# Weight sums and low weight halves made by accumulating DMAs in the output projections of a two-layer trunk

## The chip, the cores and the metric

The kernel runs on one core of one Trainium2 chip. The metric is device time in microseconds (us) of one launch. A core has TensorE (PE in the profile; its weight loads are PEld), VectorE (DVE), ScalarE (ACT), GpSimd (POOL) and SyncE (SP). Transfers are issued by an engine's queue (SPq, POOLq, ACTq) and moved by 16 DMA engines that all queues share. Those issued by SP are called hardware_dynamic in the profile, those issued by POOL software_dynamic.

## The reference, cut to what matters

One step of a diffusion trunk: 128 prompt tokens and 512 sample tokens, model width 2048, two layers. Each layer normalizes and modulates its input, projects it into heads and gates, mixes tokens (windowed attention and a short convolution in layer 0, differential and dense attention in layer 1), and sends the concatenated branches through one output projection, whose gated result is added to the input:

```
y = concat([y_first, y_second], axis=-1)   # 640 tokens x 2048
x = x + gate * (y @ w_out)                 # w_out is 2048 x 2048
```

The change is in `y @ w_out` of both layers. All arrays are float32.

## The kernel before, in words

**Exactness.** TensorE multiplies float32r. To keep float32 accuracy each operand is split into a high part (rounded by a copy into float32r) and a low part (the rest): `split` (L240 to L242) makes `hi` on ACT and `lo = x - hi` on DVE. A product takes three matmuls, high x high, high x low, low x high. `split_w` (L260) does this for 128x512 float32 of weights (four row tiles of 128x128) into `wh` and `wl`, from a pool with four buffers of each.

**Layout.** Activations are kept transposed: 16 row tiles of 128 features x 640 tokens. The tokens are cut into two halves of 320 columns (`HALF`), since an accumulator holds 512 float32.

**Output projection, single tiles.** `project_out` (L1098) makes 16 output tiles (`n`) of 128 features. Tiles 0, 1, 2 are the lead tiles: `run_tiles` loads y back from DRAM (`ydram`, tile `yin`) quarter by quarter, splits it into `h`, and runs the three tiles on each quarter as it comes. Then tiles 3 to `n0 - 1` follow one by one (L1126), each 16 row tiles x 2 halves x 3 = 96 matmuls. Their weights come in quarters of 256 KB (`load_raw`, tile `raw`, four buffers, SP queue), split three quarters ahead (`SPLIT_AHEAD`). `n0` is `N_SINGLE`: 4 in layer 0, 6 in layer 1.

**Output projection, pairs.** The other tiles are made two at a time by `run_pairs` (L431): a 2x2 block product with seven block products in place of eight. With A11, A12, A21, A22 the weight blocks (1024 rows x 128 columns, 512 KB; first index the tile, second the upper or lower half of the rows) and B11 to B22 blocks of the activations, the seven are Q1 (A11), Q2 (A12), N5 (A21 + A22), P6 (N5 + A11), P7 (A11 + A21), P4 (A22) and Q3 (P6 + A12). Each is 8 row tiles x 3 = 24 matmuls of 320 columns. The sums of activations (`T`, four forms) are made once per layer by `forms` (L1045), a generator that `advance(attn, ...)` steps through during the lead and single tiles. The sums of weights are made on DVE in `operand` (L455): N5 in two halves of 128x512 into `sx`, P6 and Q3 as 128x1024 added into `sx`, P7 as 128x1024 into `sf`. Each block of weights is loaded once per pair by SP (L438, A22 by L254).

**Order around the change.** Each engine works in program order. `ahead(s)` (L483) is called after each half product (a step) and makes the operands and splits up to three halves ahead; a split has to wait for one of the four `wh` and `wl` buffers, that is for PE to have finished four halves earlier. After each product, `after` (L490) combines accumulators on DVE in four scratch areas (`room`, tile `tables`), and `done` and `res_sum` (L1080) add the gated result to the residual `xr`, which `res_load` (L1076) fetched. In layer 0 the sum is stored by POOL (L1194) and squared for the next norm; in layer 1 it is transposed back by PE (`rows_out`, L1419), copied by ACT and stored by POOL (L1424, L1425). In layer 0 `x1_tail` (L1234) starts to fetch the sums back into freed operand buffers during the last pair.

Of the kernel before, what the change touches and what calls it, by code (L numbers as in the profile page):

```python
# [53 lines left out]
def trunk_kernel(ctx: ExitStack, tc: tile.TileContext, I: dict, O: dict):  # L54
# [185 lines left out]
    def split(hi, lo, x):  # L240
        A.activation(hi, x, AF.Copy)  # L241
        V.tensor_sub(lo, x, hi)  # L242
# [9 lines left out]
    def load_raw(w_ap, col, qd, js=(0, 4)):  # L252
        raw = wpool.tile([P, js[1] - js[0], P], F32, tag="raw", name="raw")
        nc.sync.dma_start(raw, w_ap[(qd * 4 + js[0]) * P:(qd * 4 + js[1]) * P, col:col + P]  # L254
                          .rearrange("(k p) n -> p k n", p=P))
        return raw

    mark = [None]

    def split_w(raw):  # L260
        wh = wpool.tile(raw.shape, F32R, tag="wh", name="wh")
        wl = wpool.tile(raw.shape, F32R, tag="wl", name="wl")
        split(wh, wl, raw)
        mark[0] = wl[:, 0, 0:1]
        return wh, wl

# [28 lines left out]
    def drain(queue):  # L295
        while queue:
            advance(queue, 1)
# [133 lines left out]
    def run_pairs(cols, w_ap, mov, room, begin, part, done, tail):  # L431

        ap = pools["cur"]
        W8 = KT // 2

        def load8(tag, col, k0, bufs):
            t = ap.tile([P, W8, P], F32, tag=tag, name=tag, bufs=bufs)
            nc.sync.dma_start(t, w_ap[k0 * P:(k0 + W8) * P, col:col + P].rearrange("(k p) n -> p k n", p=P))  # L438
            return t

        st8 = {}

        def load(p, name):
            if p >= len(cols):
                return
            c0, c1 = cols[p]
            if name == "A22":
                st8[p, name] = [load_raw(w_ap, c1, qd) for qd in (2, 3)]
            else:
                st8[p, name] = load8("w8", c1 if name == "A21" else c0, 8 if name == "A12" else 0, 4)  # L450

        def halves(t):
            return [t[:, 0:4, :], t[:, 4:8, :]]

        def operand(p, name):  # L455
            a = lambda n: st8[p, n]
            if name == "Q1":
                return halves(a("A11"))
            if name == "N5":
                x = st8["x"] = ap.tile([P, W8, P], F32, tag="sx", name="sx", bufs=1)  # L460
                for i in range(2):
                    V.tensor_add(halves(x)[i], halves(a("A21"))[i], a("A22")[i])
                return halves(x)
            if name == "P6":
                V.tensor_add(st8["x"], st8["x"], a("A11"))
                f = st8["f"] = ap.tile([P, W8, P], F32, tag="sf", name="sf", bufs=1)
                V.tensor_add(f, a("A11"), a("A21"))
                return halves(st8["x"])
            if name == "Q2":
                return halves(a("A12"))  # L470
            if name == "Q3":
                V.tensor_add(st8["x"], st8["x"], a("A12"))
                return halves(st8["x"])
            if name == "P7":
                return halves(st8["f"])
            return a("A22")

        MOV = {"Q1": "B11", "Q2": "B21", "N5": "T1", "P6": "T2", "P7": "T3", "P4": "T4", "Q3": "B22"}
        seq = [(p, n) for p in range(len(cols)) for n in MOV]
        ops, parts = {}, {}  # L480
        q1, z, u2, u4 = room

        def ahead(s):  # L483
            while len(parts) < min(s + SPLIT_AHEAD, 2 * len(seq)):
                i = len(parts)
                if i % 2 == 0:
                    ops[i // 2] = operand(*seq[i // 2])
                parts[i] = split_w(ops[i // 2][i % 2])

        def after(p, name, ps):  # L490
            if name == "Q1":
                A.copy(q1, ps)
                begin(p)
            elif name == "Q2":
                V.tensor_add(z, ps, q1)
                done(p, 0, 0, z)
            elif name == "N5":
                st8["n5"] = ps
            elif name == "P6":
                V.tensor_sub(u2, ps, q1)  # L500
                V.tensor_sub(u4, st8["n5"], u2)
                if p == len(cols) - 1:
                    part(p, 0, 1, u4)
            elif name == "P7":
                V.tensor_sub(z, ps, u4)
                done(p, 1, 1, z)
                V.tensor_add(u2, ps, u2)
                part(p, 1, 0, u2)
            elif name == "P4":
                done(p, 1, 0, ps)  # L510
            elif p == len(cols) - 1:
                done(p, 0, 1, ps)
            else:
                V.tensor_add(u4, ps, u4)
                done(p, 0, 1, u4)

        for n in ("A11", "A12", "A21", "A22"):
            load(0, n)
        ahead(0)
        for i, (p, name) in enumerate(seq):  # L520
            ps, rows_ = pproj.tile([P, 512], F32, tag=f"p{'ab'[i % 2]}{i // 2 % 2}", name="pq")[:, 0:HALF], mov[MOV[name]]
            for h in range(2):
                wh, wl = parts[2 * i + h]
                for j in range(4):
                    hi, lo = rows_(4 * h + j)
                    PE.matmul(ps, wh[:, j, :], hi, start=(h == 0 and j == 0), stop=False)  # L526
                    PE.matmul(ps, wh[:, j, :], lo, start=False, stop=False)  # L527
                    PE.matmul(ps, wl[:, j, :], hi, start=False, stop=(h == 1 and j == 3))  # L528
# [5 lines left out]
            if name == "Q1":  # L534
                load(p + 1, "A11")
            elif name == "P7":
                load(p + 1, "A12")
            elif name == "P4":
                load(p + 1, "A21")
                load(p + 1, "A22")  # L540
            if name in ("P6", "P7") and p == len(cols) - 1:
                tail(name)
            slot()

# [487 lines left out]
    for _ in fill0:  # L1032
        pass

    N_SINGLE = (4, 6)
    room = [tables[:, i * HALF:(i + 1) * HALF] for i in range(4)]
    W_OUT = [I["ev_w_out"][0], I["od_w_out"][0]]
    T, t1 = [], []
# [1 line left out]
    def big(tag, shape=(P, NT), dtype=F32, bufs=1):  # L1040

        n = 6 * HALF if tag[0] == "T" else 8 * P
        return pools["cur"].tile([P, n], dtype, tag=tag, name=tag, bufs=bufs)

    def forms():  # L1045

        f = None

        def load(j):
            ts = [big("w8", bufs=4)[:, 0:NT] for _ in range(2)]  # L1050
            for i in range(2):
                nc.sync.dma_start(ts[i], ydram[j + 8 * i])
            return ts

        T.clear()
        t1.clear()
        nxt = load(0)
        for j in range(8):
            (ya, yb), nxt = nxt, (load(j + 1) if j < 7 else None)
            b11, b12, b21, b22 = ya[:, 0:HALF], ya[:, HALF:NT], yb[:, 0:HALF], yb[:, HALF:NT]  # L1060
            x = big("sx")[:, 0:3 * HALF]
            if f is None:
                f = big("sf")
# [34 lines left out]
    def project_out(l, maker, finish, last, tail):  # L1098
# [3 lines left out]
        def job(n):  # L1102
            def f(pp):
                res_load(l, n)
                for i in range(2):
                    res_sum(l, n, pp[i], CS[:1] if i == 0 else CS[1:])
                yield
                finish(n)
            return f

        n0 = N_SINGLE[l]
        go_on = run_tiles([(n * P, job(n)) for n in range(3)], w, maker, order=(0, 2, 1, 3))


# [43 lines left out]
        def done(p, t, h, src):  # L1158
# [4 lines left out]
            elif n in seen:  # L1163
# [336 lines left out]
```

## Time and profile before

| | |
|---|---|
| time, median of 3 runs | 2329.14 us (2328.17 to 2330.53) |
| the profiled execution's own time | 2333.26 us |
| its span | 2331.3 us |
| granted TensorE clock, mean | 0.996 |
| data moved by DMA | 321.96 MB |
| pairs of layer 0 | from 980 us to 1130 us of the span |
| pairs of layer 1 | from 2199 us to 2328 us of the span |

The span is what the hardware profiler recorded of one execution. A row of a group reads: line, engine, operation, what it writes <- what it reads, shape, count | busy us in all, mean ns of one | idle time of the engine ahead of it and what ended most of it. A row in order of time starts with start and length in us; a bracket at its end is the idle time of the engine before it and what ended it. Matmuls are pipelined, so that their listed lengths overlap.

### The profile page before, as it was taken

How to read it: one execution, taken by the hardware profiler on the slowest of the kernel's cores; microseconds unless marked ns; L12 is line 12 of the kernel's file. 1: busy time of each engine (PE TensorE's matmuls, PEld its weight loads, DVE VectorE, ACT ScalarE, POOL GpSimd, SP SyncE). 2: the span in 40 equal slices, each digit the busy share in tenths (PEclk: the TensorE clock that was granted, in tenths of full speed). 3: DMA queues.
4: the chain of work that ended last, by engine and by line, in shares of the span. 5: the costliest groups of instructions: out<-in, count | busy, mean ns of one | idle time of the engine just before them, and what ended most of it. 6: DMA issues, size and time to landing. Idle time of an engine off the chain costs nothing.

```text
span 2331.3 us, 41439 instructions
## 1 busy us (share of the span) xinstructions
PE 2286.6 (98%) x15988; PEld 2210.0 (95%) x15988; DVE 1572.5 (67%) x3196; ACT 929.2 (40%) x1935; POOL 133.0 (6%) x181
## 2 busy tenths in 40 slices
PE   7999999999999999999999999999999999999999
PEld 5699999999999999999999999999999999999999
DVE  4559886786876663988855755755756754567576
ACT  4235442433422222544554344444334444444343
POOL 1001000000000000000010100101000001000101
PEclk9999999999999999999999999999999999999999
DMA  9984545445355443844431422413423312128642
GB/s 315 354 267 131 162 116 170 139 119 169 116 180 162 151 139 114 277 142 128 160 98 53 135 82 72 143 52 100 118 72 95 104 46 82 46 74 270 181 122 70
DMA packets 390630, 321.96 MB, mean 138 GB/s; under 512 B 18402, under 2 KB 336368, under 8 KB 389920
## 3 DMA queue, kind: packets, MB, share of 16 engines
q1 hardware_dynamic: 382496, 288.98, 40.9%
q0 software_dynamic: 7216, 28.16, 3.3%
q8 instruction: 126, 2.06, 0.4%
q10 hardware_dynamic: 720, 2.16, 0.3%
q14 instruction: 72, 0.59, 0.1%
HBM read 290.79 MB, written 28.44 MB: 137 GB/s over the span
## 4 chain that ended last, share of the span: by engine, by line
PE 88%; DMA 4%; DVE 4%; ACT 2%; issue 1%; POOL 0%; SPq 0%; ACTq 0%; DVEq 0%; POOLq 0%
PE pa L276 10%; PE pb L277 10%; PE pb L276 10%; PE pb L278 10%; PE pa L277 10%; PE pa L278 10%; PE pq L526 4%; PE pq L528 4%; PE pq L527 4%; PE T L704 2%; PE S L716 1%; PE S L718 1%; PE S L717 1%; DMA yin<-yd 1%; PE T L178 1%
## 5 line engine op out<-in xcount | busy, mean ns | idle before, releaser
L241 ACT ACTIVATE wh<-raw 128x512 fp32r<-128x512 f32 (+1 forms) x490 | 303.1, 620 | 794.7 <-PE pb L277 655.3
L242 DVE TENSOR_TENSOR wl<-raw,wh 128x512 fp32r<-128x512 f32 (+1 forms) x490 | 330.8, 676 | 351.3 <-ACT wh L241 326.1
L276 PE MATMUL pa<-h,wh 128*128 128x320 f32 x1760 | 560.6, 319 | 4.5 <-ACT h L241 3.2
L277 PE MATMUL pa<-h,wh 128*128 128x320 f32 x1760 | 547.3, 312 | 1.8 <-DVE h L242 1.8
L278 PE MATMUL pa<-h,wl 128*128 128x320 f32 x1760 | 546.4, 310 | 0.0
L278 PE MATMUL pb<-h,wl 128*128 128x320 f32 x1760 | 545.4, 310 | 0.0
L276 PE MATMUL pb<-h,wh 128*128 128x320 f32 x1760 | 545.0, 310 | 0.0
L277 PE MATMUL pb<-h,wh 128*128 128x320 f32 x1760 | 544.8, 310 | 0.0
L213 DVE SCALAR_TENSOR_TENSOR acc<-adaw,sT,acc 128x512 f32<-128x512 f32 (+1 forms) x600 | 357.4, 639 | 13.1 <-DMA adaw<-in_ada_w 12.4
L276 PEld LDWEIGHTS pa<-h,wh 128*128 128x128 f32 x1760 | 331.9, 189 | 24.0 <-issue 14.7
L277 PEld LDWEIGHTS pa<-h,wh 128*128 128x128 f32 x1760 | 332.6, 189 | 6.3 <-DVE h L242 2.7
L278 PEld LDWEIGHTS pa<-h,wl 128*128 128x128 f32 x1760 | 332.1, 189 | 1.2 <-issue 1.2
L278 PEld LDWEIGHTS pb<-h,wl 128*128 128x128 f32 x1760 | 330.8, 188 | 2.1 <-issue 2.1
L276 PEld LDWEIGHTS pb<-h,wh 128*128 128x128 f32 x1760 | 330.6, 188 | 1.0 <-issue 0.4
L277 PEld LDWEIGHTS pb<-h,wh 128*128 128x128 f32 x1760 | 330.8, 188 | 0.2
L690 ACT ACTIVATE p<-S,nm,rq 128x768 f32<-128x768 f32 (+3 forms) x120 | 101.2, 844 | 114.8 <-DVE nm L685 81.1
L526 PE MATMUL pq<-h,wh 128*128 128x320 f32 x352 | 110.0, 313 | 0.4 <-DVE xr L1083 0.4
L527 PE MATMUL pq<-h,wh 128*128 128x320 f32 x352 | 108.8, 309 | 0.0
L528 PE MATMUL pq<-h,wl 128*128 128x320 f32 x352 | 108.4, 309 | 0.0
L683 DVE TENSOR_REDUCE nm<-S 128x1 f32<-128x768 f32 (+3 forms) x120 | 91.9, 766 | 16.1 <-PE S L718 14.9
L241 ACT ACTIVATE pth<-T 128x512 fp32r<-128x512 f32 (+1 forms) x132 | 65.9, 533 | 71.4 <-PE T L704 71.3
L527 PE MATMUL pq<-T,wh 128*128 128x320 f32 x264 | 81.4, 308 | 0.0
(303 smaller groups left out, 3382.5 us busy)
## 6 DMA issues: line engine op xcount, KB each, us to landing
raw<-in_od_w_in SPq DMA_DIRECT2D x208, 256.0 KB, 2.8
raw<-in_ev_w_in SPq DMA_DIRECT2D x196, 256.0 KB, 3.0
adaw<-in_ada_w SPq DMA_DIRECT2D x192, 256.0 KB, 3.0
ada<-in_ada_w SPq DMA_DIRECT2D x14, 2048.0 KB, 11.0
adaw<-in_ada_w SPq DMA_DIRECT2D x128, 128.0 KB, 2.3
yd<-y POOLq DMA_DIRECT2D x34, 320.0 KB, 2.8
yin<-yd SPq DMA_DIRECT2D x32, 320.0 KB, 4.8
w<-yd SPq DMA_DIRECT2D x32, 320.0 KB, 4.4
```

The source lines that it names most:

```text
L213: V.scalar_tensor_tensor(out=a, in0=w, scalar=sT[:, kt, c:c + 1], in1=a, op0=ALU.mult, op1=ALU.add)
L241: A.activation(hi, x, AF.Copy)
L242: V.tensor_sub(lo, x, hi)
L276: PE.matmul(ps, wh[:, i, :], hi[:, sl], start=(j == js[0] if alone else (pos == 0 and j == 0)), stop=False)
L277: PE.matmul(ps, wh[:, i, :], lo[:, sl], start=False, stop=False)
L278: PE.matmul(ps, wl[:, i, :], hi[:, sl], start=False, stop=(j == js[1] - 1 if alone else (pos == 3 and j == 3)))
L526: PE.matmul(ps, wh[:, j, :], hi, start=(h == 0 and j == 0), stop=False)
L527: PE.matmul(ps, wh[:, j, :], lo, start=False, stop=False)
L528: PE.matmul(ps, wl[:, j, :], hi, start=False, stop=(h == 1 and j == 3))
L683: V.tensor_reduce(nm, s, axis=AX.X, op=ALU.max, negate=True)
L690: A.activation(p[:, 0:n], s, AF.Exp, scale=rsc, bias=nm, accum_out=l)
L704: PE.transpose(t[:, i * P:(i + 1) * P], p, ident)
```

## The change

Three things change.

1. While `project_out` runs, `split_w` makes `wl` in another way: ACT writes `wh`, ACT writes `wl = -wh`, and a DMA issued by POOL adds the raw weights to `wl`. This holds for the lead tiles, the fourth tile and the pairs.
2. In `run_pairs` each of the seven operands has a 512 KB buffer of its own turn (`r0` to `r5`, six in rotation) and is loaded by SP from DRAM, up to five ahead. Sums are made by accumulating DMAs issued by POOL: N5 adds A22 and P7 adds A21 from DRAM, P6 adds the N5 buffer and Q3 adds the P6 buffer. `forms` and `x1_tail` use these buffers in place of `w8`, `sx` and `sf`.
3. `N_SINGLE` is 4 in both layers, so that layer 1 has six pairs and one single tile behind its lead tiles.

```
-    mark = [None]
+    mark, by_dma = [None], [False]
...
-        split(wh, wl, raw)
+        if by_dma[0]:
+
+            A.activation(wh, raw, AF.Copy)
+            A.activation(wl, wh, AF.Copy, scale=-1.0)
+            nc.gpsimd.dma_start(wl, raw, accum_op=ALU.add)
+        else:
+            split(wh, wl, raw)
...
+        def src8(col, k0):
+            return w_ap[k0 * P:(k0 + W8) * P, col:col + P].rearrange("(k p) n -> p k n", p=P)
+
+        turn = [0]
+
+        def load(p, name):
+
+            c0, c1 = cols[p]
+            col, k0, add = {"Q1": (c0, 0, None), "Q2": (c0, 8, None), "N5": (c1, 0, (c1, 8)), "P6": (c0, 0, "N5"),
+                            "P7": (c0, 0, (c1, 0)), "P4": (c1, 8, None), "Q3": (c0, 8, "P6")}[name]
+            t = ops[p, name] = big(f"r{turn[0] % 6}").rearrange("p (k n) -> p k n", k=W8)
+            turn[0] += 1
+            nc.sync.dma_start(t, src8(col, k0))
+            if add is not None:
+                nc.gpsimd.dma_start(t, src8(*add) if isinstance(add, tuple) else ops[p, add], accum_op=ALU.add)
...
         def ahead(s):
+            while len(ops) < min((s + 1) // 2 + 5, len(seq)) and len(ops) < len(parts) // 2 + 6:
+                load(*seq[len(ops)])
             while len(parts) < min(s + SPLIT_AHEAD, 2 * len(seq)):
                 i = len(parts)
-                if i % 2 == 0:
-                    ops[i // 2] = operand(*seq[i // 2])
-                parts[i] = split_w(ops[i // 2][i % 2])
+                h = ops[seq[i // 2]][:, i % 2 * 4:i % 2 * 4 + 4, :]
+                parts[i] = split_w(h)
...
-    N_SINGLE = (4, 6)
+    N_SINGLE = (4, 4)
...
         n0 = N_SINGLE[l]
+        by_dma[0] = True
...
         drain(prep)
+        by_dma[0] = False
...
-        for k in (range(0, 4) if name == "P6" else range(4, 6)):
-            x1_back(k, big("w8", bufs=4) if k < 4 else big("sx" if k == 4 else "sf"))
+        for k in {"P6": (0, 1, 2, 3), "P7": (4,), "P4": (5,)}[name]:
+            x1_back(k, big(f"r{k}"))
```

More of the change, by code (lines that the diff above doesn't have):

```diff
@@ L434, in run_pairs @@
         W8 = KT // 2
[L436 to L439, printed above, removed]
-        st8 = {}
[L443 to L476, printed above, removed]
@@ L478, in run_pairs @@
-        MOV = {"Q1": "B11", "Q2": "B21", "N5": "T1", "P6": "T2", "P7": "T3", "P4": "T4", "Q3": "B22"}
+        def src8(col, k0):
[10 more added lines that the diff above has]
+                nc.gpsimd.dma_start(t, src8(*add) if isinstance(add, tuple) else ops[p, add], accum_op=ALU.add)
@@ L479, in run_pairs @@
+        MOV = {"Q1": "B11", "Q2": "B21", "N5": "T1", "P6": "T2", "P7": "T3", "P4": "T4", "Q3": "B22"}
+        st8 = {}
         seq = [(p, n) for p in range(len(cols)) for n in MOV]
@@ L515, in after @@
                 done(p, 0, 1, u4)
-        for n in ("A11", "A12", "A21", "A22"):
-            load(0, n)
         ahead(0)
@@ L533, in run_pairs @@
             ahead(2 * i + 2)
[L534 to L541, printed above, removed]
+            if name in ("P6", "P7", "P4") and p == len(cols) - 1:
                 tail(name)
@@ L1049, in load @@
         def load(j):
-            ts = [big("w8", bufs=4)[:, 0:NT] for _ in range(2)]
+            ts = [big(f"r{j % 2 * 2 + i}")[:, 0:NT] for i in range(2)]
             for i in range(2):
@@ L1060, in forms @@
             b11, b12, b21, b22 = ya[:, 0:HALF], ya[:, HALF:NT], yb[:, 0:HALF], yb[:, HALF:NT]
-            x = big("sx")[:, 0:3 * HALF]
+            x = big("r4")[:, 0:3 * HALF]
             if f is None:
-                f = big("sf")
+                f = big("r5")
             d = room[j] if j < 4 else f[:, (j - 4) * HALF:(j - 3) * HALF] if j < 7 else b11
```

## The prediction

> **What bounds the kernel now.** I read four views: busy times and slices of the page, then the groups by line, then a table of time windows (us from the span's start, busy time of each engine with its instructions, granted clock, share of the 16 DMA engines, GB/s), then instructions in order of time inside one pair.
>
> ```profile
> PE 2286.6 (98%) x15988; PEld 2210.0 (95%) x15988; DVE 1572.5 (67%) x3196; ACT 929.2 (40%) x1935; POOL 133.0 (6%) x181
> ...
> L526 PE MATMUL pq<-h,wh 128*128 128x320 f32 x352 | 110.0, 313 | 0.4 <-DVE xr L1083 0.4
> L527 PE MATMUL pq<-h,wh 128*128 128x320 f32 x352 | 108.8, 309 | 0.0
> L528 PE MATMUL pq<-h,wl 128*128 128x320 f32 x352 | 108.4, 309 | 0.0
> ```
> ```profile
> 1003.30:1027.90 24.60, 24.60 (x170) 24.60 (x169) 20.55 (x35) 10.50 (x18) 1.06 (x2) 1.00 0.47 140
> ...
> 2171.00:2199.00 28.00, 28.00 (x194) 27.80 (x193) 13.43 (x25) 9.81 (x20) 2.57 (x4) 1.00 0.48 136
> ...
> 2250.00:2275.70 25.70, 25.70 (x180) 25.68 (x179) 19.15 (x33) 10.54 (x19) 2.57 (x4) 1.00 0.44 132
> ```
>
> TensorE bounds it. Columns after the length are PE, PEld, DVE, ACT, POOL, clock, DMA share, GB/s. The first window is one pair of layer 0, the last one pair of layer 1, the middle one two single tiles of layer 1. PE is never idle in them and the clock is full. DVE is the next engine (20.55 of 24.60 us), yet PE waited for it 0.4 us in all pairs together. So whatever is taken off DVE in the pairs is worth at most that. DMA is below half.
>
> One trap: a matmul's listed 309 ns is not its price, as matmuls overlap. A pair is 7 products x 8 row tiles x 3 = 168 matmuls in 24.60 us, 0.146 us each.
>
> **The change part by part.**
>
> *Six pairs instead of five in layer 1.* Two single tiles (2 x 96 matmuls) become one pair (168): 24 matmuls at 0.146 us, **-3.5 us**. This is the whole gain in sight, since the row transposes and residual sums of a tile stay the same.
>
> *DVE.* Per pair 14 subtractions, two half sums and three whole sums go. They lay beside PE; I cost them at **0** (at most the 0.4 us above). Nothing that PE waits for is behind them.
>
> *ACT.* Each split gets a second activation.
>
> ```profile
> 976.84 1.15 ACT L241 ACTIVATE wh<-w 128x512 fp32r<-128x512 f32 x2 [1.02 <-DMA w<-in_ev_w_out]
> ```
>
> Two back to back take 1.15 us, so 14 more add 14 x 0.575 = 8.1 us to ACT's 10.50 in a pair: 18.6 of 24.60. It fits, **0**. In the lead tiles three more of them stand before the activations that make `h`, 1.7 us per unit of 10.5 us of matmuls; hidden while DMA lasts longer there, and it does (below).
>
> *POOL.* It issues all accumulating DMAs, in order.
>
> ```profile
> 1003.28 0.54 POOL L1194 DMA_DIRECT2D xd<-xr  x1 [21.34 <-DVE xr L1083]
> ...
> 2247.96 0.76 POOL L1424 DMA_DIRECT2D out_y_sample<-ot  x1 [20.36 <-ACT ot L1423]
> ```
>
> An issue of 128 rows takes 0.54 us, one of 512 pieces 0.76. A sum from DRAM has 1024 pieces; by the same slope 1.05 us. A pair gets 16 x 0.54 + 2 x 1.05 = 10.7 us of issues more: room enough. But the DMA that makes operand N5, P6, P7 or Q3 waits on POOL for its plain load to land, and the `wl` DMAs of the coming steps, and the stores of `xr`, stand behind it.
>
> *The path from a free buffer to wl.* Before, `wl` came 0.7 us behind `wh`. Now it is ACT, ACT, POOL, DMA.
>
> ```profile
> 1040.66 0.19 PEld L526 LDWEIGHTS pq<-T,wh 128*128 128x128 f32 x1
> ...
> 1040.92 0.63 ACT L241 ACTIVATE wh<-sf 128x512 fp32r<-128x512 f32 x1 [1.13 <-PE pq L527]
> ...
> 1040.95 0.19 PEld L528 LDWEIGHTS pq<-T,wl 128*128 128x128 f32 x1
> ...
> 1042.62 0.64 ACT L241 ACTIVATE wh<-raw 128x512 fp32r<-128x512 f32 x1 [1.07 <-PE pq L527]
> ```
> ```profile
> yd<-y POOLq DMA_DIRECT2D x34, 320.0 KB, 2.8
> ...
> xd<-xr POOLq DMA_DIRECT2D x16, 320.0 KB, 3.6
> ...
> out_new_c_k<-kg POOLq DMA_DIRECT2D x8, 64.0 KB, 1.9
> ```
>
> A half product (step) lasts 12 x 0.146 = 1.76 us. The split of the part for step n+3 starts 0.26 us into step n, when PE releases the buffer (four buffers; the bracket shows ACT already waits for that). PE wants `wl` 0.29 us into step n+3, that is 3 x 1.76 + 0.29 = 5.57 us after step n began. The path is 0.26 + 1.15 + landing. No row shows an accumulating DMA; plain stores from POOL land 1.9 us (64 KB) to 3.6 us (320 KB) after issue. For 256 KB I take 2.9: 4.3 us. It fits, with **1.3 us to spare**, if nothing is ahead of it in the queue.
>
> *DMA bytes.* Here it does not fit. Per pair, before: four operands of 0.524 MB, two residuals in and two out of 0.328 MB, 3.4 MB (140 GB/s x 24.6 us agrees). After: seven operand loads and two sums from DRAM (4.72 MB), two sums from SBUF (1.05), 14 `wl` of 0.262 MB (3.67), residuals and stores (1.31): **10.75 MB**. In 24.6 us that is 437 GB/s.
>
> ```profile
> 58.00:116.00 58.00, 52.96 (x368) 37.06 (x369) 29.07 (x66) 16.64 (x31) 0.00 (x0) 0.97 1.01 355
> 10.00:20.00 10.00, 7.00 (x33) 5.38 (x34) 5.07 (x14) 4.97 (x9) 1.14 (x2) 0.93 1.02 398
> ```
> ```profile
> q0 software_dynamic: 7216, 28.16, 3.3%
> ```
>
> Where all 16 engines are busy they moved 355 GB/s over 58 us, 398 at best. So a pair takes at least 10.75 / 0.398 = 27.0 us. Counted by busy shares instead: before, 0.47 x 24.6 = 11.6 us of full engines, 297 GB/s; the 2.62 MB more from DRAM at that rate are 8.8 us, the 4.72 MB inside SBUF at POOL's rate (28.16 MB in 3.3% of 2331.3 us: 366 GB/s) 12.9; sum 33.3 us. These are the prices if an accumulating byte costs what a plain one does.
>
> It can hardly cost that: a sum needs its destination read too, which is a second pass over 5.77 MB. With it, 16.5 MB per pair: 41.5 us at 398 GB/s, 46.5 at 355, by the shares (33.3 + 5.77 at about 355) 49.6. The upper end would be that each accumulating DMA is served alone: 14 x 2.9 + 4 x 3.6 = 55 us. Between 27.0 and 55 I take **41.5 us**: two passes at the best rate that the trace shows, since nearly half the first pass and all of the second stay in SBUF.
>
> The Trainium skill ("Collectives: The Full Stack", The bandwidth ceiling) says of adding transfers that the addition is free but the two source reads share one ring, and gives 32.35 against 62.28 GB/s for the copy, a factor of 1.93. No run here shows that yet; by it the two-pass price holds and the one-pass price does not.
>
> *Lead tiles and the fourth tile.* Their 16 quarters per layer also get `wl` by DMA, 4.19 MB, 8.4 with two passes.
>
> ```profile
> 966.00:980.00 14.00, 14.00 (x97) 13.95 (x96) 13.57 (x30) 9.14 (x17) 1.31 (x3) 1.00 0.99 313
> 2113.00:2124.00 11.00, 11.00 (x77) 11.00 (x77) 6.97 (x10) 6.41 (x10) 0.00 (x0) 1.00 0.81 284
> 2124.00:2135.00 11.00, 11.00 (x77) 11.00 (x77) 9.26 (x17) 4.89 (x7) 0.00 (x0) 1.00 0.91 285
> 2135.00:2146.00 11.00, 10.45 (x71) 10.18 (x71) 9.83 (x16) 5.73 (x9) 0.00 (x0) 1.00 0.95 305
> 2146.00:2157.00 11.00, 10.42 (x74) 10.15 (x73) 10.41 (x22) 4.22 (x7) 1.06 (x2) 1.00 0.85 262
> 2157.00:2171.00 14.00, 13.76 (x96) 13.50 (x95) 9.55 (x18) 5.08 (x9) 2.82 (x5) 1.00 1.04 329
> ```
>
> DMA is already full there: the 58 us of layer 1 leave (11 x 0.48 + 14 x -0.04) = 4.7 us of engines free, layer 0, with a like last stretch, I put at the same. 8.4 MB at 398 GB/s are 21 us; 21 - 4.7 = 16 us per layer, **+32 us** in two (one pass: 10.5 - 4.7, +12).
>
> *Sum, against the profiled execution* (2333.26 us, its span 2331.3 with 2.0 around it): layer 0 pairs 6 x (41.5 - 24.6) = +101; layer 1 pairs 6 x (41.5 - 25.7) = +95; lead tiles +32; sixth pair -3.5. Together +225, or 2558. The median of the runs shown, 2329.14, is 4 us below the profiled one, so I say **2554 us**.
>
> **The rivals.**
>
> *One pass, and the queue.* Accumulating costs what copying does. Then a pair is 27.0 to 33.3 us by bytes, and the look-ahead adds: four operand sums per pair stand ahead of a `wl` with an issue of 0.54 to 1.05 us and 0.524 / 0.398 = 1.3 us of transfer; beyond the 1.3 us to spare each costs PE about 1 us. At 31 (27.0 + 4) to 33.3 us: 6 x (6.4 to 8.7) + 6 x (5.3 to 7.6) + 12 - 3.5, which is +79 to +106: about **2420**. For it: packet times of DRAM loads may overlap with SBUF traffic (share 1.04 above). Against: the destination must be read.
>
> *Served one by one.* If an accumulating DMA holds the software queue until it lands, 55 us per pair: 6 x 30.4 + 6 x 29.3 + 32 - 3.5 = +386, **2715**. For it: one POOL queue, in order, with waits for loads inside. Against: q0's stores now move at 366 GB/s.
>
> *It hides.* The other side: the engines deliver the 437 GB/s, and each accumulating DMA lands within 2.9 + 1.3 = 4.2 us of its issue; from there on PE waits for nothing in the pairs, only -3.5 us is left, **2326**. It decides at 437 GB/s in the pair windows. Against: the best 10 us of this trace had 398. By the Trainium skill ("DMA: Bandwidth & Descriptors", Where 436 GB/s comes from) the 16 ports allow 435 GB/s, which would make a one-pass pair 24.7 us and is this rival; the trace's 398 is below it.
>
> **How the numbers follow.** Forecast (two passes) 0.50, its own range 2500 to 2625 (41.5 less a tenth, to 46.5 us per pair). One pass 0.27, one by one 0.14, hidden 0.09. The range runs from 2395 (one pass with 30 us per pair) to 2690; left out are the hidden case and most of the one-by-one case. About 0.2% (4.7 us) is what a measurement of this kernel can tell from no change. -3.5 us is inside it: same 0.06.
>
> ```profile
> L276 PE MATMUL pa<-h,wh 128*128 128x320 f32 x1760 | 560.6, 319 | 4.5 <-ACT h L241 3.2
> L277 PE MATMUL pa<-h,wh 128*128 128x320 f32 x1760 | 547.3, 312 | 1.8 <-DVE h L242 1.8
> ```
>
> To be faster, part of the 3.2 + 1.8 us that PE waits for `h` in the lead tiles would have to go as well: 0.03. Slower 0.91.
>
> **What would show it.** In the pair windows the DMA share should be near 1.0, a pair last about 41 us, PE idle ahead of L528 with `wl` and a DMA as releaser, DVE fall from 20.6 us per pair to about 6, ACT rise to about 18.6. Software queue bytes should go from 28 to about 106 MB (200 `wl` and 48 operand sums). Landing of `wl` well above 4.2 us shows the look-ahead broken. Wrong would be: a DMA share below 0.9 with PE idle (then it is the queue's order or latency, not bytes), or PE without idle time in the pairs (it hides).

## The result and the profile after

The changed kernel takes **2652.62 us** (median of four runs, 2650.25 to 2654.87) where the kernel before takes 2329.84 (2328.17 to 2331.46): a ratio of 1.139 with a 95% interval of 1.137 to 1.140. Its profiled execution took 2654.87 us, with a span of 2651.9. The forecast was 2554, range 2395 to 2690.

Some lines have moved: the pairs' matmuls are now L506 to L508 (before L526 to L528), the lead tiles' L282 to L284, `wh` and `-wh` on ACT L265 and L266, the DMA that completes `wl` L267, an operand's load L454, its sum L456.

From the page after: busy times, the software queue, four groups (busy us, mean ns | idle before it and what ended it), and the landing of `wl` (median us from issue).

```profile
PE 2382.2 (90%) x15964; PEld 2283.2 (86%) x15964; DVE 1405.3 (53%) x2954; ACT 1055.1 (40%) x2142; POOL 367.9 (14%) x429
...
q0 software_dynamic: 64432, 105.77, 20.8%
...
L284 PE MATMUL pb<-h,wl 128*128 128x320 f32 x1728 | 537.3, 311 | 5.7 <-DMA wl<-raw 5.7
...
L508 PE MATMUL pq<-h,wl 128*128 128x320 f32 x384 | 143.3, 376 | 122.2 <-DMA wl<-r 122.0
...
L267 POOL DMA_DIRECT2D wl<-r x168 | 176.0, 1337 | 156.6 <-ACT wl L266 146.3
L508 PE MATMUL pq<-T,wl 128*128 128x320 f32 x288 | 102.9, 358 | 74.6 <-DMA wl<-r 74.5
...
wl<-r POOLq DMA_DIRECT2D x168, 256.0 KB, 7.7
```

PE, never idle in the pairs before, now waits 122.2 + 74.6 = 196.8 us there ahead of the one matmul that reads `wl`, and what ends the wait is the DMA that completes `wl`. It lands 7.7 us after its issue, where the path had room for 4.2. In the lead tiles (L284) the same wait is small.

The table of time windows after: one pair of layer 0, then one stretch of layer 1.

```profile
1093.60:1142.30 48.70, 31.17 (x171) 29.33 (x171) 7.34 (x15) 19.21 (x32) 18.27 (x21) 0.86 1.09 222
...
2440.00:2490.00 50.00, 32.50 (x178) 31.18 (x178) 5.70 (x13) 19.17 (x33) 20.00 (x22) 0.84 1.02 205
```

A pair takes 48.7 us instead of 24.6. DVE has fallen to 7.3 us and ACT risen to 19.2. PE is idle for 17.5 us, and its busy time has grown too, from 24.6 to 31.2 us for the same 168 matmuls: the clock column stands at 0.86. So of 24.1 us more, 17.5 are waits and 6.6 are PE at a slower clock.

The clock in steps of 2 us, with PE's weight loads there in order of time (the bracket is the wait before).

```profile
1064.00:1066.00 2.00, 2.00 (x16) 2.00 (x15) 0.61 (x2) 1.47 (x3) 0.00 (x0) 1.00 1.15 310
1066.00:1068.00 2.00, 1.30 (x9) 1.03 (x8) 0.43 (x1) 1.50 (x3) 1.65 (x3) 1.00 0.71 139
1068.00:1070.00 2.00, 0.59 (x4) 0.59 (x5) 0.00 (x0) 0.19 (x1) 1.85 (x3) 1.00 1.06 197
1070.00:1072.00 2.00, 2.00 (x10) 2.00 (x8) 0.00 (x0) 0.33 (x1) 0.00 (x0) 0.52 1.04 172
1072.00:1074.00 2.00, 1.22 (x5) 0.82 (x5) 0.00 (x0) 0.93 (x2) 0.74 (x1) 0.50 1.13 189
...
1078.00:1080.00 2.00, 2.00 (x16) 2.00 (x15) 0.98 (x2) 1.27 (x2) 0.47 (x1) 1.00 1.14 300
```
```profile
1066.85 0.19 PEld L507 LDWEIGHTS pq<-h,wh 128*128 128x128 f32 x1
1069.40 0.19 PEld L508 LDWEIGHTS pq<-h,wl 128*128 128x128 f32 x1 [2.37 <-DMA wl<-r]
...
1070.64 0.33 PEld L506 LDWEIGHTS pq<-h,wh 128*128 128x128 f32 x1
1070.91 0.33 PEld L507 LDWEIGHTS pq<-h,wh 128*128 128x128 f32 x1
```

After a wait of 2.37 us the granted clock falls to 0.50, and the loads follow each other at 0.27 us instead of 0.146.

One pair seen from POOL, in order of time, shows the order that the queue imposes.

```profile
1112.51 0.85 POOL L267 DMA_DIRECT2D wl<-r  x1 [7.25 <-PE pq L507]
1114.89 0.85 POOL L456 DMA_DIRECT2D r<-r  x1 [1.53 <-DMA r<-in_ev_w_out]
1115.42 2.98 POOL L267 DMA_DIRECT2D wl<-r  x3
...
1130.43 1.57 POOL L456 DMA_DIRECT2D r<-in_ev_w_out  x1 [4.52 <-issue]
```

POOL stands at the sum until the operand's plain load has landed; then three `wl` DMAs come in one burst behind it.

**The sum.** By the start of one sum to the start of the same sum of the next pair, a pair of layer 0 takes 48.6 us (1066.35 to 1260.86 over four pairs) and one of layer 1 51.6 (2415.40 to 2621.95). Six pairs of layer 0 are 6 x 24.0 = 144 us more; six pairs of layer 1 stand in place of five of 25.7 and two single tiles of 28.0 together, 309.6 - 156.5 = 153. By this count 26 of the 323 us are left for the lead and fourth tiles and the edges. But the pairs at the ends are not as long as those between. From the first matmul of the pairs to the start of their last one, layer 0 takes 295.4 us (989.9 to 1285.3) instead of 149.8 (980.2 to 1130.0), which is 145.6 more. Layer 1 takes 300.5 (2346.2 to 2646.7) instead of 129.3 (2197.1 to 2326.4) and 28.0 for the two single tiles, which is 143.2 more. So about 32 of the 320.6 us between the two spans lie outside the pairs: 9.7 ahead of those of layer 0, and 21.8 between the two layers' pairs once the two single tiles are taken out.

### The profile page after: what moved, and what is told of

The parts are those of the page before. It is cut to its first block, busy times and chain, and to the rows that moved or that the text cites. A ratio compares the mean times of both kernels' runs of the same rounds, so it can differ in the third digit from the quotient of the medians.

```text
span 2651.9 us, 41966 instructions
## 1 busy us (share of the span) xinstructions
PE 2382.2 (90%) x15964; PEld 2283.2 (86%) x15964; DVE 1405.3 (53%) x2954; ACT 1055.1 (40%) x2142; POOL 367.9 (14%) x429
## 3 DMA queue, kind: packets, MB, share of 16 engines
q0 software_dynamic: 64432, 105.77, 20.8%
## 4 chain that ended last, share of the span: by engine, by line
PE 65%; DMA 24%; DVE 4%; issue 3%; ACT 2%; POOL 1%; SPq 0%; POOLq 0%; ACTq 0%; DVEq 0%
DMA wl<-r 9%; PE pa L282 8%; PE pb L282 8%; PE pb L283 8%; PE pb L284 8%; PE pa L283 8%; PE pa L284 8%; DMA r<-in_ev_w_out 4%; DMA r<-in_od_w_out 4%; PE T L677 2%; DMA r<-yd 1%; PE S L689 1%; PE S L691 1%; PE S L690 1%; PE T L178 1%
## 5 line engine op out<-in xcount | busy, mean ns | idle before, releaser
L282 PE MATMUL pa<-h,wh 128*128 128x320 f32 x1728 | 551.3, 320 | 9.5 <-ACT h L241 8.2
L241 ACT ACTIVATE wh<-raw 128x512 fp32r<-128x512 f32 (+1 forms) x428 | 264.2, 619 | 736.6 <-PE pb L283 625.2
L283 PE MATMUL pa<-h,wh 128*128 128x320 f32 x1728 | 538.7, 312 | 4.6 <-DVE h L242 4.4
L284 PE MATMUL pb<-h,wl 128*128 128x320 f32 x1728 | 537.3, 311 | 5.7 <-DMA wl<-raw 5.7
L284 PE MATMUL pa<-h,wl 128*128 128x320 f32 x1728 | 537.0, 311 | 3.3 <-DMA wl<-raw 3.3
L282 PE MATMUL pb<-h,wh 128*128 128x320 f32 x1728 | 537.3, 311 | 0.0
L283 PE MATMUL pb<-h,wh 128*128 128x320 f32 x1728 | 536.6, 311 | 0.0
L242 DVE TENSOR_TENSOR wl<-raw,wh 128x512 fp32r<-128x512 f32 (+1 forms) x428 | 288.4, 675 | 333.0 <-ACT wh L241 308.3
L282 PEld LDWEIGHTS pa<-h,wh 128*128 128x128 f32 x1728 | 326.1, 189 | 30.5 <-issue 14.7
L284 PEld LDWEIGHTS pb<-h,wl 128*128 128x128 f32 x1728 | 326.4, 189 | 8.5 <-DMA wl<-raw 6.4
L284 PEld LDWEIGHTS pa<-h,wl 128*128 128x128 f32 x1728 | 326.4, 189 | 5.4 <-DMA wl<-raw 4.1
L282 PEld LDWEIGHTS pb<-h,wh 128*128 128x128 f32 x1728 | 326.2, 189 | 1.0 <-issue 0.4
L508 PE MATMUL pq<-h,wl 128*128 128x320 f32 x384 | 143.3, 376 | 122.2 <-DMA wl<-r 122.0
L265 ACT ACTIVATE wh<-r 128x512 fp32r<-128x512 f32 x168 | 105.7, 631 | 354.9 <-PE pq L507 320.1
L508 PEld LDWEIGHTS pq<-h,wl 128*128 128x128 f32 x384 | 90.7, 237 | 132.4 <-DMA wl<-r 132.3
L267 POOL DMA_DIRECT2D wl<-r x168 | 176.0, 1337 | 156.6 <-ACT wl L266 146.3
L508 PE MATMUL pq<-T,wl 128*128 128x320 f32 x288 | 102.9, 358 | 74.6 <-DMA wl<-r 74.5
L506 PE MATMUL pq<-h,wh 128*128 128x320 f32 x384 | 139.7, 364 | 0.7 <-DVE xr L1056 0.7
```

Source lines behind the costliest of these rows:

```text
L265: A.activation(wh, raw, AF.Copy)
L267: nc.gpsimd.dma_start(wl, raw, accum_op=ALU.add)
L282: PE.matmul(ps, wh[:, i, :], hi[:, sl], start=(j == js[0] if alone else (pos == 0 and j == 0)), stop=False)
L283: PE.matmul(ps, wh[:, i, :], lo[:, sl], start=False, stop=False)
L284: PE.matmul(ps, wl[:, i, :], hi[:, sl], start=False, stop=(j == js[1] - 1 if alone else (pos == 3 and j == 3)))
```

## The experiments

Two theories stood at the start: **full engines** (the bytes of all transfers, destination reads included, fill the 16 DMA engines) and **the queue** (the accumulating DMAs go through one software queue in order, behind waits, and land too late, though the engines have room). A third comes from the critical chain inside a pair after the change (start us, us, what):

```profile
1097.88 10.01 DMA wl<-r
...
1107.95 6.40 DMA r<-in_ev_w_out
...
1115.96 7.12 DMA wl<-r
...
1123.23 6.06 DMA r<-in_ev_w_out
```

It runs from a load through its sum to `wl` and on to the next load, three times per pair: **the loop** (an operand's buffer is released by the DMA that reads it, which lets the next load start).

Each is compared with the kernel before on its own chip; lengths of pairs are those of layer 0, from sum to sum. The diffs are against the kernel before for e1, e4, e8 and e12, and against the changed one for the others.

### e1: six pairs alone

```
-    N_SINGLE = (4, 6)
+    N_SINGLE = (4, 4)
```

> The kernel before with only the sixth pair in layer 1 (single tiles 4 and 4); all sums and low halves stay on VectorE. Both theories of the loss (full DMA engines, or the order of the software queue) expect the 24 matmuls less and nothing else: 3.5 us less, about 2326 us. Rival: VectorE, busy 20.6 of 24.6 us in a pair, or the sums of activations that now have to be ready two tiles earlier, hold TensorE up in layer 1: 2329 us or more, with idle time of TensorE at the start of the pairs.

2334.70 us against 2333.01, ratio 1.0005 (0.9996 to 1.0015). The 3.5 us are not there. Time windows of it around the start of layer 1's pairs, then DVE's work on the first operand in order of time:

```profile
2155.00:2165.00 10.00, 9.02 (x53) 9.02 (x54) 9.37 (x21) 6.55 (x16) 3.88 (x6) 0.83 0.96 291
...
2170.00:2175.00 5.00, 2.68 (x18) 2.23 (x16) 3.15 (x5) 0.63 (x1) 0.00 (x0) 1.00 0.38 97
```
```profile
2171.84 1.29 DVE L462 TENSOR_TENSOR sx<-w,raw 128x512 f32<-128x512 f32 x2 [2.94 <-DMA w<-in_od_w_out]
```

By this trace the two single tiles had been cover. DVE makes the forms beside the lead tiles (9.37 of 10 us busy) and the first operands' loads must wait for the buffers that the forms use; with one single tile left PE arrives earlier, loses about 1 us, then 2.3, and the clock dips to 0.83. These waits and the clock are of the size of the 24 matmuls saved. That the missing cover is the cause is argued from the trace: e8 and e12, below, were to relieve DVE there, and neither brought the gain.

### e2: sums by DMA, wl on DVE

```
-        by_dma[0] = True
```

> The changed kernel with the low halves back on VectorE; the four weight sums of a pair stay accumulating DMAs, loads and buffers as changed. Full engines: the loads (3.67 MB per pair) and four sums of 0.52 MB at the 163 GB/s that the software queue's added bytes took in the changed kernel are 17 + 13 = 30 us of full engines per pair, 27.6 us with the share of 1.08 that was seen there; 3 to 5 us per pair over 24.6 to 25.7, so 2360 to 2390 us. Queue order: TensorE waits for no software DMA but through operands that are made five ahead, so nothing is late: about 2326 us.

2409.52 us, ratio 1.032 (1.030 to 1.034); a pair 31.2 us. The engines' share is 1.04 between 1060 and 1160 us. What PE waits for in e2 (us in all, times, longest):

```profile
PE pq L506 <- ACT wh L241: 44.5, 15, 11.4
```

Few waits (15) but long: `wh` has to wait until an operand's load or sum has landed. Neither theory had this number: the nearer one was off by 19.5 us.

### e3: plain copies in place of all accumulating DMAs

```
-            nc.gpsimd.dma_start(wl, raw, accum_op=ALU.add)
+            nc.gpsimd.dma_start(wl, raw)
...
-                nc.gpsimd.dma_start(t, src8(*add) if isinstance(add, tuple) else ops[p, add], accum_op=ALU.add)
+                nc.gpsimd.dma_start(t, src8(*add) if isinstance(add, tuple) else ops[p, add])
```

> The changed kernel with every accumulating DMA turned into a plain copy of the same source to the same place (so the low halves and the sums are not computed; instructions, waits, queue and bytes written stay). Full engines with two passes per accumulated byte: one pass goes, 33.3 us of full engines per pair by the prices of the kernel before, 31 us at a share of 1.08; about 2400 to 2440 us. Queue order and waits: the same waits and the same order, so still above 2580 us.

2520.06 us, ratio 1.080 (1.079 to 1.082); a pair 39.6 us. The software queue from 1060 to 1160 us (packets, MB, share of 16 engines), of the changed kernel, then of e3; then the landing of `wl` on e3's page:

```profile
q0 software_dynamic: 9249, 13.19, 76.8%
```
```profile
q0 software_dynamic: 6855, 16.20, 53.8%
```
```profile
wl<-r POOLq DMA_DIRECT2D x168, 256.0 KB, 5.4
```

13.19 MB in 76.8 us of full engines are 172 GB/s, 16.20 in 53.8 are 301: **a byte of the software queue costs 1.75 times as much when it is accumulated.** That is 9.0 of the 24.0 us that a pair lost. The other 15 remain with plain copies, at a share of only 0.95 and with PE still idle, so full engines and the second pass cannot be all.

### e4: wl by DMA, sums on DVE

```
+        if by_dma[0]:
+            A.activation(wh, raw, AF.Copy)
+            A.activation(wl, wh, AF.Copy, scale=-1.0)
+            nc.gpsimd.dma_start(wl, raw, accum_op=ALU.add)
+        else:
+            split(wh, wl, raw)
...
-    N_SINGLE = (4, 6)
+    N_SINGLE = (4, 4)
```

> The kernel before with six pairs and only the low halves made by ACT and accumulating DMAs; weight sums on VectorE, four operand loads per pair as before. Full engines: 14 x 0.262 MB at 163 GB/s are 22.5 us, with 11.6 us for the rest 34 us of full engines, 31.6 us per pair at a share of 1.08; with the lead tiles 2430 to 2460 us. Queue order: no operand sum and no wait for a load stands ahead of a low half on GpSimd, the path of 4.3 us fits into the 5.6 us: 2326 to 2345 us (lead tiles alone).

2483.94 us, ratio 1.065 (1.063 to 1.066); a pair 35.2 us. Landing of `wl` on e4's page, by its source:

```profile
wl<-sx POOLq DMA_DIRECT2D x72, 256.0 KB, 4.5
...
wl<-raw POOLq DMA_DIRECT2D x56, 256.0 KB, 4.6
wl<-w POOLq DMA_DIRECT2D x48, 256.0 KB, 5.5
```

No sum and no wait for a load stands in the queue here, and the engines' share is 0.90, yet `wl` lands later than the 4.2 us that the path allows. The parts do not add up: over 24.6 us, e2 costs 6.6 and e4 10.6 per pair, both together 24.0. Sums in the queue make the late `wl` later. Nor is all of e4's loss the landing: between 1010 and 1190 us ACT waited 35.7 us, in five waits, for DVE's sum in `sx`, and DVE 38.6 us, in six, for the `wl` DMA that still reads `sx`.

### e6: half of wl accumulated

```
-            nc.gpsimd.dma_start(wl, raw, accum_op=ALU.add)
+            nc.gpsimd.dma_start(wl[:, 0:2], raw[:, 0:2], accum_op=ALU.add)
```

> The changed kernel with each low half's DMA covering two of its four row tiles (the other two keep minus the high part, so the output is not the reference's); as many DMAs, waits and issues, half the added bytes of wl. Full engines: 1.83 MB per pair less at 163 GB/s are 11 us of 52.6 us of full engines, so 38 to 39 us per pair in place of 48.7, and 2500 to 2530 us. Queue order: a landing is shorter by about 1 of 7.3 us, three steps ahead; at most 0.4 us per step, 5 us per pair, so above 2590 us.

2577.85 us, ratio 1.106 (1.104 to 1.109); a pair 44.9 us. The landing of `wl` on its page:

```profile
wl<-r POOLq DMA_DIRECT2D x168, 128.0 KB, 6.3
```

Half of the bytes of `wl` gone saves 3.7 us per pair and 1.4 us of landing. So most of the landing is not the DMA's own bytes. The result lies between the two expectations.

### e7: sums issued later

The sum of an operand is issued by POOL two operands after its load, so that the load should have landed.

```
+            while sums and (sums[0][0] <= (s + 1) // 2 + 3 or 2 * sums[0][0] <= len(parts) + 4):
+                _, t, src = sums.pop(0)
+                nc.gpsimd.dma_start(t, src, accum_op=ALU.add)
```

> The changed kernel with the four operand sums of a pair issued two operands later on GpSimd than their loads on SyncE, so that the load has landed when GpSimd comes to the sum and nothing behind it waits; the same bytes. Full engines: no change, 2640 to 2665 us. Queue order: the 156 us that GpSimd waits for loads ahead of its sums go, 8 us or more per pair, so below 2560 us.

2660.30 us, ratio 1.141 (1.139 to 1.144). POOL's waits at the sums in the changed kernel, then in e7 (us in all, times, longest):

```profile
POOL r L456 <- DMA r<-in_od_w_out: 97.1, 20, 9.8
POOL r L456 <- DMA r<-in_ev_w_out: 58.7, 19, 5.0
```
```profile
POOL r L469 <- DMA r<-in_ev_w_out: 83.8, 18, 11.2
POOL r L469 <- DMA r<-in_od_w_out: 83.5, 18, 10.1
```

The wait was to go and did not (155.8 us, then 167.3): the loads themselves start late. So this run does not tell the theories apart.

### e8 and e12: more room for the sixth pair

e8 is e1 with one subtraction of the forms on POOL; e12 is e1 with the four `wl` of layer 1's single tile made by accumulating DMAs.

```
-            V.tensor_sub(d, b11, b12)
+            G.tensor_sub(d, b11, b12)
```
```
-                parts.append(split_w(raws[len(parts)]))
+                parts.append(split_w(raws[len(parts)], l == 1))
```

> The kernel before with six pairs in layer 1 and one of the four differences of each activation form moved from VectorE to GpSimd, to relieve VectorE where the pairs of layer 1 begin (it was 94% busy there with six pairs alone, and TensorE lost the 3.5 us by waits of 2.3 and 2.0 us and a lower granted clock). If VectorE's backlog at that place ate the gain: 2 to 3.5 us less than with six pairs alone, about 2330 us beside 2333 for the kernel before. If not: the same as with six pairs alone, or more, where GpSimd is late.

> The kernel before with six pairs, and in layer 1 only the four low halves of the single tile ahead of the pairs made by ACT and accumulating DMAs (look-ahead three quarters, 10.5 us). If VectorE's backlog there (8.4 of 9 us, then 5.0 of 5 us busy) held the operand buffers of the first pair too long: 1 to 3 us less than with six pairs alone, 2328 to 2331 us beside 2331. If the full DMA engines of that stretch decide (share 0.96 to 1.10): no gain, or a few us more.

e8: 2340.24 us, ratio 1.0037 (1.0021 to 1.0053). e12: 2340.89, ratio 1.0041 (1.0028 to 1.0054). Both are slower than e1's 1.0005. PE's weight loads of e12 in order of time, those that wait:

```profile
2168.63 0.19 PEld L283 LDWEIGHTS pb<-h,wl 128*128 128x128 f32 x1 [1.66 <-DMA wl<-raw]
2180.74 0.19 PEld L533 LDWEIGHTS pq<-h,wl 128*128 128x128 f32 x1 [3.30 <-DVE wl L242]
```

DVE's relief bought a wait for a DMA of 1.66 us, and the wait for the first operand stayed. No run found a version that beats the kernel before; e1 equals it.

### e9: extra loads that missed their place

```
             turn[0] += 1
             nc.sync.dma_start(t, src8(col, k0))
+            nc.sync.dma_start(tables[:, 1280:1536].rearrange("p (k n) -> p k n", k=2), src8(col, k0)[:, 0:2, :])
```

> The changed kernel with a useless load of 0.131 MB on SyncE beside each operand load, 0.92 MB per pair into columns that nobody reads; GpSimd's queue stays as it is. Full engines: 0.92 MB at 297 GB/s are 3.1 us of full engines, 2.9 us per pair at a share of 1.08: 30 to 40 us longer than the changed kernel, 2680 to 2695 us. Queue order: the engines have room, at most a few us more, below 2665 us.

2667.25 us, ratio 1.144 (1.142 to 1.146); a pair 48.8 us, as without them. It looks like proof against full engines. But the extra loads' own line (duration, first and last start us) says that they were not there:

```profile
L455 SPq DMA_DIRECT2D tables<-in_ev_w_out x42: 367/368/500, 583.8 to 701.6; - x42
L455 SPq DMA_DIRECT2D tables<-in_od_w_out x42: 367/368/1880, 2214.9 to 2437.6; - x42
```

Nothing tied them to the pairs, so they were placed early: all of layer 0's are 280 us ahead of its pairs. The run says nothing on the pairs of layer 0; e13 replaces it.

### e10 and e11: buffers released early

e10: the DMA that completes `wl` reads a fixed piece of `T` instead of the operand, so ACT, not the DMA, releases the operand's buffer. e11: also the sums from SBUF read a fixed piece.

```
-            nc.gpsimd.dma_start(wl, raw, accum_op=ALU.add)
+            nc.gpsimd.dma_start(wl, raw if src is None else src, accum_op=ALU.add)
...
-                parts[i] = split_w(h)
+                parts[i] = split_w(h, T[0][:, 0, 0:512].bitcast(F32).rearrange("p (k n) -> p k n", k=4))
```

> The changed kernel, but in the pairs each low half's DMA adds a fixed piece of an activation form in place of the raw weights (the output is not the reference's); same bytes, same count, same queue. What changes is that an operand buffer is free as soon as ACT has made the high parts, and no longer when the low half has landed. Dependency loop (low half lands 7 to 10 us, then its buffer's next load 6.4 us, then the sum on GpSimd that waits for that load, then the next low half; three turns of 16 us per pair): the loop is cut, loads start some 8 us earlier, 36 to 42 us per pair, 2490 to 2570 us. Full engines: nothing changes, 2640 to 2665 us.

> As the run with the fixed source for the low halves, and the two operand sums from SBUF also add fixed pieces (no sum waits for another sum; the output is not the reference's); same bytes. Dependency loop: a second chain, the sum N5 landing in 8 us before P6's sum may start, goes too; 0 to 5 us per pair less than with the low halves' source alone. Full engines: the same as the changed kernel, 2640 to 2665 us.

e10: 2627.03 us, ratio 1.127 (1.125 to 1.128), a pair 47.3. e11: 2631.02, ratio 1.129 (1.127 to 1.131). In e11 the sums move against the pairs, so that from sum to sum a pair reads 45.5; from the first `wl` matmul of the second pair to that of the sixth it is 47.1, where e10 has 47.2 and the changed kernel 48.5. The landing of `wl` on e10's page:

```profile
wl<-T POOLq DMA_DIRECT2D x168, 256.0 KB, 8.1
```

The loop through the buffers is worth about 25 us of 323, though the critical chain ran through it. Cut open, the chain closes elsewhere: `wl` lands even later. The loop theory falls as the main cause. e11 adds nothing to e10, so the second chain, from sum to sum, is worth nothing that can be told here.

### e13: useless traffic inside the pairs

```
                 parts[i] = split_w(h)
+                nc.scalar.dma_start(spare[i % 8], h[:, 0:2, :].rearrange("p k n -> p (k n)"))
```

> The changed kernel, and behind each split of the pairs ScalarE's queue stores two of the four row tiles of the operand (128 rows of 1 KB) to a spare place in DRAM that nothing reads: 14 useless stores, 1.83 MB, per pair. They wait for nothing that the split has not waited for, so they lie in the pairs, unlike the extra loads of e9, which the trace shows at 583.8 to 701.6 and 2214.9 to 2437.6 us, ahead of most of the pairs, so that e9 said nothing of them. In the pairs of the changed kernel the accumulating and storing packets of the software queue hold 76.8% of the 16 engines and those of the hardware queue 30.9%, 52.4 of 48.7 us. Theory of full engines: 1.83 MB at the hardware queue's rate there (8.76 MB in 30.9% of 100 us, 283 GB/s) are 6.5 us more of engine time, a pair takes about 54.7 us, the kernel 2700 to 2740. Theory of the software queue alone (one queue in order, the engines have room): pairs stay within 1 us of 48.7, under 2668.

2680.71 us against 2328.67, ratio 1.152 (1.150 to 1.154). In layer 0 a pair takes 52.1 us (1068.89 to 1277.31 over four), 3.5 more than without the stores. Layer 1 from 2415.4 to 2596.7 us, three and a half pairs in both kernels: the changed one, then e13.

```profile
DMA packets 42140, 37.01 MB, mean 204 GB/s; under 512 B 1693, under 2 KB 33682, under 8 KB 42132
...
q0 software_dynamic: 16048, 22.23, 74.3%
q1 hardware_dynamic: 26084, 14.68, 29.0%
```
```profile
DMA packets 48725, 43.51 MB, mean 240 GB/s; under 512 B 2468, under 2 KB 40149, under 8 KB 48717
...
q0 software_dynamic: 16062, 22.35, 70.1%
q1 hardware_dynamic: 25824, 14.83, 28.5%
q10 hardware_dynamic: 6831, 6.23, 10.7%
```

In layer 1 the engines carried 6.5 MB more in the same time, and a pair stayed at 51.6 us. There they had room, at a share that read 1.03 before and 1.09 now. In layer 0 (share 1.08 before) the stores cost about half of the 6.5 us that full engines would give.

Those 3.5 us cannot be put down to the engines alone, since ACT, whose queue issues the stores, was held up too. ACT's waits in four pairs of layer 0 of e13 (us in all, times, longest), then all of them in four pairs of the changed kernel:

```profile
ACT wh L265 <- PE pq L508: 48.8, 37, 4.0
ACT wh L265 <- DMA r<-in_ev_w_out: 31.4, 7, 6.4
ACT wl L266 <- DMA r<-in_ev_w_out: 21.0, 5, 6.0
ACT wl L266 <- DMA r<-r: 11.6, 4, 6.0
```
```profile
ACT wh L265 <- PE pq L507: 116.5, 52, 10.2
ACT sq L1165 <- DVE xr L1056: 0.2, 1, 0.2
```

In the changed kernel ACT waits there for PE alone; in e13 it waits 64.0 us for operands' DMAs. L266 reads nothing but `wh`, so its 32.6 us can only be those of a store ahead of it in ACT's order. So the stores did wait for more than the splits did, against what was expected of them. The landing of `wl` hardly grew: 7.7 us, then 7.9 in layer 0; 8.7, then 7.9 in the stretch of layer 1.

By the first and last matmuls of the pairs, of the 25.6 us between the two spans 20.6 lie in layer 0's pairs, 4.3 in layer 1's, 2.0 between them, and -1.3 ahead. **Neither theory got its number: 2680.7 lies between 2668 and 2700.** Full engines are not the bound in layer 1; whether sharing them costs anything in layer 0 is not shown.

## Why the prediction was right or wrong

**Bound and direction: right.** PE bounds the kernel before, and the work taken off DVE was worth nothing: DVE fell from 20.6 to 7.3 us per pair ("about 6" was named), and PE gained none of it. ACT's 18.6 us came out at 19.2 and it fits. The software queue moved 105.77 MB, "about 106". PE is idle ahead of the `wl` matmul with the DMA as releaser.

**The sixth pair, -3.5 us: wrong.** e1 shows 0 (+1.7, interval -0.9 to +3.5). I counted matmuls. By e1's trace the step that failed is that the two single tiles were taken to be worth only their matmuls, while they were also cover for the forms and the first operands; no run shows that cause by itself.

**The path to wl, 1.3 us to spare: the step that failed in size.** I gave the landing 2.9 us, from plain stores. The fastest of all accumulating DMAs took 3.2 (4.3 + 0.3: still in time), the median was 7.7. The text said "if nothing is ahead of it in the queue", and then priced what is ahead only in the one-pass rival (4 us per pair), and at nothing in the forecast. It did say that a landing well above 4.2 us would show the look-ahead broken, and that is what came. The same path with the measured median landings gives the step: three steps plus 0.29 us must hold 0.26 + 1.15 + landing, so a step is (landing + 1.12) / 3, and a pair 14 of them:

| kernel | median landing of wl, us | pair by it | ACT + until issue + landing, means | pair by these | pair measured |
|---|---|---|---|---|---|
| the room there was | 4.2 | 24.8 | | | 24.6 (before) |
| e4 | about 4.8 | 27.6 | 1.41 + 0.32 + 4.92 | 30.9 | 35.2 |
| e3 | 5.4 | 30.4 | 1.31 + 1.54 + 5.25 | 37.7 | 39.6 |
| e6 | 6.3 | 34.6 | 1.31 + 1.65 + 6.21 | 42.7 | 44.9 |
| changed kernel | 7.7 | 41.2 | 1.31 + 1.85 + 7.78 | 50.9 | 48.6 |
| e10 | 8.1 | 43.0 | 1.31 + 1.40 + 7.98 | 49.7 | 47.3 |

By the median landing alone, 16.6 of the 24.0 us follow, but for e4 only 3.0 of 10.6: the path lacks a term. The traces have it. The means follow every split through four pairs of layer 0 (56 splits). In the changed kernel ACT takes 1.31 us for `wh` and `-wh`, then 1.85 us pass until POOL issues the DMA (0.29 at the least), and the DMA lands after 7.78. I had 1.15, nothing and 2.9. The three together stand in place of 1.15 + landing.

But for e4, where ACT also waits for DVE's sums, the path so measured comes within 2.4 us of each pair. So a pair of the changed kernel lasts about as long as three steps of look-ahead need for a late `wl`: the landing is the larger part, the wait on POOL ahead of the issue the smaller. The slower clock (6.6 us) is not needed as a term of its own; whether it adds anything to the waits is not shown.

**POOL's issues: mis-sized; what that cost was not separated from POOL's waits.** An accumulating DMA of 128 rows holds POOL for 0.85 us, not 0.54, and a sum from DRAM for 1.57, not 1.05. That is 18.2 us per pair with the stores, and fits into 48.7.

**DMA bytes, two passes, 41.5 us: the right sign, too cheap, and only part of the cause.** Two passes at 398 GB/s put an accumulated byte at 199; in the pairs the software queue ran at 172, and 1.75 times the plain price (e3). The Trainium skill ("Collectives: The Full Stack", The bandwidth ceiling) gives 1.93 for adding transfers; the measured 1.75 is near it. The count by busy shares (49.6) came closer than my choice (41.5), since in the trace q0's packets do hold 76.8% of the engines. But 41.5 and 49.6 were both priced as a bound on bytes, and e13 moved 18% more bytes through layer 1's pairs in the same time. So the step that failed is that the engines' bytes set the length of a pair, and that 49.6 is near 48.6 is luck. My own test, "a share near 1.0", could not tell a limit from a busy reading.

**Lead tiles, +32 us: met in the sum, not in its halves.** About 32 us lie outside the pairs, but 9.7 in layer 0 and 21.8 in layer 1 in place of 16 each. Layer 0 was not like layer 1: before the change its DMA share was 0.66 from 900 to 966 us, and only the last 14 us were full. PE waits there for `wl` only 5.7 + 3.3 us in the whole kernel (on the two accumulators), so what the 32 us consist of stays open. Layer 1's stretch is as full as predicted: 2280.00 to 2355.50 us at a share of 0.99 with PE busy 59.6 of 75.5 us.

**The clock: missing.** I held PE's price at 0.146 us per matmul. Behind waits of a few us it is 0.27 for some us; PE's busy time grows by 6.6 us per pair, or about 80 us in all. How much of it adds to the waits is open, as said above. The Trainium skill ("TensorE: Matmul & The Clock Gate", What's actually happening) says that the clock is halved after an idle window of about 3.4 us; here the half clock follows a wait of 2.37 us, while after one of 2.41 us that ended at 1145.81 the clock stayed at 1.00 until 1152. So here the length of one wait does not decide it.

**The rivals.** One pass (2420) is refuted by e3: even plain copies take 2520. One by one (2715) is refuted in its price of 55 us per pair, yet right in that the queue's order matters. Hidden is refuted. The time came out at 2652.62, inside the range and 28 us above the forecast case's own (2500 to 2625). The direction, the wait for `wl` and its releaser were foreseen; that the time lies inside the range is in part luck. The forecast put 196 us on the pairs as a bound on bytes and nothing on a late `wl`; the pairs lost 289, and `wl` was what PE waited for.

**What stays open.** How the landing of 7.7 us divides between the packets' own time in the queue, the burst behind a sum and shared engines: e3 (accumulating or not, 2.3 us), e6 (own bytes, 1.4) and e4 (no sums, about 2.9) overlap and do not add up. The trace of the changed kernel shows the order of the queue: none of the 168 `wl` DMAs landed ahead of one that POOL had issued before it. 127 of them were issued while the sum of an operand was still under way in the queue and landed after 8.5 us (median), the other 41 after 5.4. That compares DMAs within one run and is no experiment. A look-ahead of four or more steps would test the path by itself; it needs more `wh` and `wl` buffers and was not tried.

## What to carry to other kernels

When a step of a tuned pipeline is handed to DMA, price its latency against the look-ahead in steps, with everything that stands ahead of it in the same queue, before counting bytes: 3.5 us late per operand half cost more here than DVE's whole relief could have given. A DMA share near 1 is no proof of a limit; add traffic to see, and look in the trace whether that traffic ran where it should. And the tiles next to a pipeline's start can be cover for its set-up: here taking two away (e1) gained nothing of the 3.5 us that their matmuls were worth.

## What the runs showed of the hardware that was not expected

- An accumulating DMA of 128 rows holds POOL's issue for 0.85 us where the same transfer as a plain copy takes 0.53 (e3), a sum from DRAM 1.57 against 0.90, and its packets hold the engines 1.75 times as long per byte (172 against 301 GB/s).
- The share of the 16 engines can read 1.09 and the bytes still rise: 204 to 240 GB/s in e13.
- The granted clock went to 0.50 after a wait of 2.37 us and came back to 1.00 within 8 us (the window from 1078 us reads 1.00); after a wait of 2.41 us that ended at 1145.81 it read 1.00 until 1152.
- The DMAs that POOL issued landed in the order of issue: of the 168 `wl` DMAs of the changed kernel none overtook an earlier one.
